# High and low activations in one moving operand, and the MLP's activations moved by 192 bytes

## The chip, the cores and the metric

The kernel runs on one core of one Trainium2 chip. The metric is the device time of one execution in microseconds, the median of several. The profile is that of one execution.

## What is computed

The reference is one layer of a hybrid decoder over 256 tokens of width 2048, in float32:

```python
h = rms_norm(x, pre_mix_norm[l])
gq, gk, gv, gz, ga, gb, mq, mk, mv = jnp.split(h @ w_in[l], split_at, axis=-1)
y_gdn = gdn_branch(gq, gk, gv, gz, ga, gb, conv_w[l], a_log[l], dt_bias[l], gdn_norm_w[l])
y_moba = moba_branch(mq, mk, mv)
mix = jnp.concatenate([y_gdn, y_moba], axis=-1) @ w_out[l]
x = x + rms_norm(mix, post_mix_norm[l])
ca = memory_cross_attention(rms_norm(x, pre_mem_norm[l]), rms_norm(mem, mem_kv_norm[l]),
                            w_mq[l], w_mk[l], w_mv[l], w_mo[l])
x = x + rms_norm(ca, post_mem_norm[l])
f = jnp.square(jax.nn.relu(rms_norm(x, pre_mlp_norm[l]) @ w_up[l])) @ w_down[l]
x = x + rms_norm(f, post_mlp_norm[l])
```

The mixer has 8 heads of a gated delta rule (with a short convolution and silu on q, k and v) and 8 heads of causal softmax attention (one block of 256 tokens). The cross attention has 4 heads over 256 memory tokens, the MLP a hidden width of 8192.

## The kernel before

**Products in parts.** Every matrix product runs in float32r in three parts: each float32 operand is split into a high part, its cast to float32r, and a low part, what is left of it. The product is high x high + high x low + low x high. The weights come from memory in units of 512 KB ([128 partitions, 1024 columns] of float32), in the order of their use (`Stream`, lines 53 to 83): a load on the queue of SP, the cast to the high part `whi` on ScalarE (line 69), the subtraction that gives the low part `wlo` on VectorE (line 71). There are five buffers of raw units and four each of high and low parts, and units are issued three ahead of the one in use.

**Two kinds of product.** In a transposed product the weights are the stationary operand and the activations the moving one, so the result is [128 columns of the product, 256 tokens]. `a_tile` (line 107) makes one such tile of 128 columns in 16 steps, one for each block of 128 rows; `a_group` (line 118) makes four tiles at once, row block by row block, while the activations still arrive. Each step is `three` (line 102): the high weights times the high activations `act[0][k]`, the high weights times the low ones `act[1][k]`, the low weights times the high ones, each with 256 moving columns. In an untransposed product, `b_group` (line 134), the activations are stationary and 512 columns of weights move; it also has three matmuls a step.

Transposed products are: the mixer's k, q, v, z projections and q, k of its block attention (activations x0), the memory's k (activations m0) and q (activations h1) of the cross attention, and all of the MLP's first matrix (activations h2). Untransposed are the attention's v, both output projections, the memory's v and the MLP's second matrix.

**Activations.** `xslot` (line 226) makes two tiles of [128, 16, 256] for high and low parts. `norm_split` (line 222) fills them: the high part on ScalarE, the low part on VectorE. The results of the MLP's first matrix, after relu and square (`up_out`, line 894), are split in the same way into four tiles of eight blocks, one named f and three named fp, which the second matrix reads as stationary operands.

**What takes the tiles out of the banks.** Each tile of a transposed product ends in half a bank, [128, 256]. In the mixer one VectorE instruction multiplies it by the tokens' scales and writes it out: line 341 for k, q and v (`normed`), lines 689 and 690 for the block attention, line 698 for z; line 826 does it for the memory's k, ScalarE's line 863 for the queries of the cross attention. In `up_out` ScalarE's relu reads the bank, VectorE squares, ScalarE casts the high part and VectorE subtracts for the low one.

**Order.** TensorE's order is written by hand: after each unit of weights `tick` lets each generator in the list `bg` do its next step (Gram matrices, the triangular inverse, the delta rule, the softmaxes, transposes of a residual), so its small products stand between the units. On the other engines a scheduler sets the order.

Of the kernel before, what the change touches and what calls it, by code (L numbers as in the profile page):

```python
# [7 lines left out]
F32 = mybir.dt.float32  # L8
F32R = mybir.dt.float32r
I32 = mybir.dt.int32  # L10
AF = mybir.ActivationFunctionType
OP = mybir.AluOpType
# [24 lines left out]
def layer(ctx, tc, xT, xn, memT, cols, rows, wab, win, wout, wmq, wmk, wmv, wmo, wup, wdn, out):  # L37
# [15 lines left out]
    class Stream:  # L53
        """the weights in the order of their use, loaded and split in two float32r parts ahead of it"""
# [47 lines left out]
    def three(o, whi, wlo, act, k, first, last):  # L102
        mm(o, whi, act[0][k], start=first, stop=False)
        mm(o, whi, act[1][k], start=False, stop=False)
        mm(o, wlo, act[0][k], start=False, stop=last)

    def a_tile(act):
        """128 columns, transposed: [column, token]"""
        o = mmps()[:, :T]
        k = 0  # L110
        while k < KT:
            for w in ws.next():
                three(o, *w, act, k, k == 0, k == KT - 1)
                k += 1
            tick()
        return o

    def a_group(act, order, pre=None):
        """512 columns, transposed, over rows as they arrive"""
        o = [mmps()[:, :T] for _ in range(4)]  # L120
# [13 lines left out]
    def b_group(act, kts, last=False, banks=None):  # L134
        """512 columns, as they are: [token, column], the tokens in two blocks"""
# [37 lines left out]
    def newton8(a, name, quarter=None):  # L173
        """-8 / sqrt(a) for columns of sums: each step leaves -2 times its estimate"""
# [50 lines left out]

    def xslot(name):
        hl = [ap_.tile([P, KT, T], F32R, tag="x" + i, name=name + i) for i in "hl"]
        return [[a[:, k] for k in range(KT)] for a in hl]
# [14 lines left out]

    def row_load(pool, tag, i):
        """a norm's weights on every partition, for the scale that newton8 leaves"""
# [17 lines left out]
    def col_sum(sq, name):  # L263
        """1 / root mean square by token, from squares [column, token] summed over the blocks of columns"""
# [6 lines left out]
    hx = xslot("x0")  # L271
    with tc.tile_pool(name="ld", bufs=1) as ld:
# [29 lines left out]
        def ab_tile():  # L302
# [3 lines left out]
            for k in range(KT):  # L306
                three(o, wa[1][:, k], wa[2][:, k], hx, k, k == 0, k == KT - 1)
# [18 lines left out]
    with tc.tile_pool(name="p1", bufs=1) as p1:  # L326
# [11 lines left out]
        def normed(o):  # L338
            c = xcs[count[0] % 4]
            count[0] += 1  # L340
            V.tensor_tensor(c[:, 3:], o, r0b[0], OP.mult)
            return c

        def conv_silu2(c, ch, dst):
            """twice the silu of the convolved channels"""
# [17 lines left out]
        def square_sums(x, dst, h):  # L363
            """the sums over the channels, for each token: columns h and H + h of dst"""
# [81 lines left out]
        def inverse():  # L446
            """the inverses of the 32 x 32 diagonal blocks of I - N, then of the 64s and the 128s"""
# [57 lines left out]
        def level(j0):  # L505
# [3 lines left out]
            for l in range(2):  # L509
                # left: the columns of the first block of each pair, right: those of the second  # L510
# [60 lines left out]
        def gate_rows(q):  # L571
            """the heads' outputs by the inverse root of their mean squares, four heads at a time"""
# [82 lines left out]
        def begin(o_ab):  # L655
            """what follows from the first group once the tokens' scales are there"""
# [18 lines left out]
        for what, h in TURNS:  # L675
# [11 lines left out]
            if what == "m":  # L687
                q, k = t1(), t1()
                V.scalar_tensor_tensor(q, a_tile(hx), QS, r0b[0], OP.mult, OP.mult)
                V.tensor_tensor(k, a_tile(hx), r0b[0], OP.mult)  # L690
# [4 lines left out]
            if what == "z":  # L695
                o = a_tile(hx)
                zs[h] = zt[:, h] if h < 5 else t1()
                V.tensor_tensor(zs[h], o, r0b[0], OP.mult)
# [9 lines left out]
    xp = ctx.enter_context(tc.tile_pool(name="xp", bufs=1))  # L708
    x1 = xp.tile([P, KT, T], F32, tag="x1", name="x1")
    with ExitStack() as es:  # L710
# [6 lines left out]
        def stat_out(o, c, dst, copy):  # L717
            """the squares' sums of 512 columns, and the columns themselves out of the way"""
# [7 lines left out]
        def residual(src, last, wcol, ncol, act, name, lag):  # L726
            """x1 += rms norm of [src, last], transposed; its split for the next product"""
# [299 lines left out]
```

## Time and profile before

| | us |
|---|---|
| median of 3 runs | 1337.73 |
| lowest and highest of them | 1337.37, 1339.63 |
| span of the profiled execution | 1334.2 |
| TensorE matmuls, busy | 1313.6 |
| VectorE, busy | 836.7 |
| ScalarE, busy | 646.8 |

The profiled execution has one span, from its first to its last instruction. It is 3.5 us below the median of the runs, which also holds what lies around it. A matmul's end is modelled, and matmuls overlap, so two rows of matmuls are read by the distance of their starts. The profile names instructions by line, by the tile written and by the tiles read: `mm<-h2h,whi` is a matmul into a bank mm from the high activations h2h and the high weights whi.

### The profile page before, as it was taken

Reading aid. Unit: us, or ns where it says so; the run is one execution under the profiler, and the core shown is the slowest. Engines: PE = TensorE matmul, PEld = TensorE weight load, DVE = VectorE, ACT = ScalarE, POOL = GpSimd, SP = SyncE. Lnnn points to the kernel's source line nnn. Section 1 sums busy time; section 2 is a strip of 40 time slices with the busy share of each in tenths; the row PEclk is TensorE's granted clock in tenths of the full one; section 3 lists DMA queues with packets and bytes.
Section 4 is the critical chain, followed back from the end, with each engine's and each line's share of the span. In section 5 each row is a group of like instructions: output and inputs, shape, how many; then the busy total and the mean of one; then the engine's idle time right before and its main releaser. Section 6 shows DMA issues by size and latency. Waiting matters only on the chain.

```text
span 1334.2 us, 22207 instructions
## 1 busy us (share of the span) xinstructions
PE 1313.6 (98%) x8845; PEld 1211.1 (91%) x8845; DVE 836.7 (63%) x1408; ACT 646.8 (48%) x975; POOL 35.3 (3%) x64
## 2 busy tenths in 40 slices
PE   7999999999999999999999999999999999999996
PEld 7899989999997889889999998888899999888886
DVE  8887769767565769669755554444455555554555
ACT  7544444425445756667544444344444444443442
POOL 1010010100000000000000000000000000000000
PEclk9999999999999999999999999999999999999998
DMA  8465555724347855535555555555555555655552
GB/s 309 159 183 176 187 187 166 206 96 143 129 157 277 283 184 187 207 126 185 188 181 185 180 188 187 191 188 189 188 184 182 186 180 187 217 189 190 189 187 86
DMA packets 72248, 246.49 MB, mean 185 GB/s; under 512 B 10392, under 2 KB 11728, under 8 KB 71760
## 3 DMA queue, kind: packets, MB, share of 16 engines
q1 hardware_dynamic: 69872, 239.27, 54.2%
q0 software_dynamic: 2272, 5.80, 1.7%
q8 instruction: 69, 1.13, 0.3%
q14 instruction: 35, 0.29, 0.1%
HBM read 241.35 MB, written 3.69 MB: 184 GB/s over the span
## 4 chain that ended last, share of the span: by engine, by line
PE 93%; DMA 3%; DVE 2%; ACT 1%; issue 1%; SPq 0%; DVEq 0%; ACTq 0%; POOLq 0%
PE mm L49 86%; PE ax L49 7%; DMA xs<-in_memT_dram 1%; DVE wlo L71 0%; PE ax L750 0%; ACT whi L69 0%; DMA wraw<-in_wout_dram 0%; DMA t<-rd 0%; DVE ca L950 0%; DMA wraw<-in_win_dram 0%; DMA rd<-t 0%; ACT m0h L223 0%; SPq L713 0%; PE ax L620 0%; PE ax L540 0%
## 5 line engine op out<-in xcount | busy, mean ns | idle before, releaser
L71 DVE TENSOR_TENSOR wlo<-wraw,whi 128x1024 fp32r<-128x1024 f32 (+1 forms) x434 | 528.2, 1219 | 372.2 <-ACT whi L69 371.7
L69 ACT ACTIVATE whi<-wraw 128x1024 fp32r<-128x1024 f32 (+1 forms) x434 | 455.3, 1052 | 497.4 <-PE mm L49 282.1
L49 PE MATMUL mm<-h2h,whi 128*128 128x256 f32 x1024 | 290.3, 283 | 0.0
L49 PE MATMUL mm<-h2l,whi 128*128 128x256 f32 x1024 | 289.9, 283 | 0.0
L49 PE MATMUL mm<-h2h,wlo 128*128 128x256 f32 x1024 | 289.9, 283 | 0.0
L49 PE MATMUL mm<-whi,fp 128*128 128x512 f32 (+1 forms) x816 | 244.0, 382 | 0.0
L49 PE MATMUL mm<-x0h,whi 128*128 128x256 f32 x768 | 223.6, 291 | 6.8 <-ACT whi L69 6.8
L49 PE MATMUL mm<-x0h,wlo 128*128 128x256 f32 x768 | 218.3, 284 | 0.0
L49 PE MATMUL mm<-x0l,whi 128*128 128x256 f32 x768 | 218.2, 284 | 0.0
L49 PEld LDWEIGHTS mm<-h2l,whi 128*128 128x128 f32 x1024 | 196.6, 192 | 0.1
L49 PEld LDWEIGHTS mm<-h2h,whi 128*128 128x128 f32 x1024 | 196.6, 192 | 0.0
L49 PEld LDWEIGHTS mm<-h2h,wlo 128*128 128x128 f32 x1024 | 196.6, 192 | 0.0
L49 PEld LDWEIGHTS mm<-whi,fp 128*128 128x128 f32 x816 | 149.9, 188 | 32.6
L49 PE MATMUL mm<-wlo,fp 128*128 128x512 f32 (+1 forms) x408 | 155.7, 382 | 0.0
L49 PEld LDWEIGHTS mm<-x0h,whi 128*128 128x128 f32 x768 | 148.2, 193 | 7.3 <-ACT whi L69 6.8
L49 PEld LDWEIGHTS mm<-x0l,whi 128*128 128x128 f32 x768 | 148.3, 193 | 0.5
L49 PEld LDWEIGHTS mm<-x0h,wlo 128*128 128x128 f32 x768 | 148.1, 193 | 0.2 <-DVE wlo L71 0.2
L49 PEld LDWEIGHTS mm<-wlo,fp 128*128 128x128 f32 x408 | 76.7, 188 | 16.2
L49 PE MATMUL mm<-whi,f 128*128 128x512 f32 (+1 forms) x272 | 81.1, 377 | 0.0
L49 PEld LDWEIGHTS mm<-whi,f 128*128 128x128 f32 x272 | 50.1, 188 | 9.6
L897 ACT ACTIVATE fp<-ft 128x256 fp32r<-128x256 f32 x48 | 20.0, 418 | 65.1 <-DVE ft L896 65.1
L49 PE MATMUL mm<-wlo,f 128*128 128x512 f32 (+1 forms) x136 | 51.3, 378 | 0.0
(368 smaller groups left out, 1445.9 us busy)
## 6 DMA issues: line engine op xcount, KB each, us to landing
wraw<-in_wup_dram SPq DMA_DIRECT2D x128, 512.0 KB, 4.2
wraw<-in_wdn_dram SPq DMA_DIRECT2D x128, 512.0 KB, 3.9
wraw<-in_win_dram SPq DMA_DIRECT2D x110, 512.0 KB, 4.3
wraw<-in_wout_dram SPq DMA_DIRECT2D x32, 512.0 KB, 4.8
wraw<-in_wmk_dram SPq DMA_DIRECT2D x8, 512.0 KB, 4.3
wraw<-in_wmq_dram SPq DMA_DIRECT2D x8, 512.0 KB, 3.8
wraw<-in_wmv_dram SPq DMA_DIRECT2D x8, 512.0 KB, 4.8
wraw<-in_wmo_dram SPq DMA_DIRECT2D x8, 512.0 KB, 4.0
```

Of the source, the lines that this page charges most:

```text
L49: TE.matmul(o, l, r, start=start, stop=stop, skip_group_check=skip)
L69: cast = S.activation(hi, r, AF.Copy)
L71: sub = V.tensor_tensor(lo, r, hi.bitcast(F32), OP.subtract)
L897: S.activation(f[:, 0, j], t, AF.Copy)
```

## The change

A pair of activations now lies side by side: `xslot` makes one tile [128, 16, 2, 256], in which the high and the low 256 columns of a row block follow each other, and `parts` hands out three views of it, high, low, and both as 512 columns. `three` has two matmuls: the high weights times both, 512 columns, into a whole bank, and the low weights times the high activations, 256 columns, onto its left half. The right half then holds high weights x low activations. Whatever takes a tile out of its bank first has ScalarE copy the right half (`right`) and VectorE add the left half to it. In `up_out` the copy stands in the relu's place, and the relu and the square are one VectorE instruction. The small product of the decays, `ab_tile`, keeps its three matmuls. A tile of 48 float32 (192 bytes in each partition) ahead of the MLP's buffers moves them: the three fp tiles' addresses leave 64 bytes over a multiple of 256 where they left 128. The addresses of f, of the inputs' tiles and of the weights' buffers leave 64 before and after.

```diff
     def three(o, whi, wlo, act, k, first, last):
-        mm(o, whi, act[0][k], start=first, stop=False)
-        mm(o, whi, act[1][k], start=False, stop=False)
-        mm(o, wlo, act[0][k], start=False, stop=last)
+        mm(o, whi, act[2][k], start=first, stop=False)
+        mm(o[:, :T], wlo, act[0][k], start=False, stop=last)
+
+    def right(o):
+        t = sm.tile([P, T], F32, tag="right", name="right", bufs=2)
+        S.activation(t, o[:, T:], AF.Copy)
+        return t
...
-        o = mmps()[:, :T]
+        o = mmps()
...
-        o = [mmps()[:, :T] for _ in range(4)]
+        o = [mmps() for _ in range(4)]
...
+    def parts(*tiles):
+        ks = [a[:, k] for a in tiles for k in range(a.shape[1])]
+        return [[k[:, 0] for k in ks], [k[:, 1] for k in ks], [k.rearrange("p i t -> p (i t)") for k in ks]]
+
     def xslot(name):
-        hl = [ap_.tile([P, KT, T], F32R, tag="x" + i, name=name + i) for i in "hl"]
-        return [[a[:, k] for k in range(KT)] for a in hl]
+        return parts(ap_.tile([P, KT, 2, T], F32R, tag="x", name=name))
...
+    def scaled(dst, o, by, const=1.0):
+        t = right(o)
+        V.tensor_tensor(t, o[:, :T], t, OP.add)
+        V.scalar_tensor_tensor(dst, t, const, by, OP.mult, OP.mult)
...
-            V.tensor_tensor(c[:, 3:], o, r0b[0], OP.mult)
+            scaled(c[:, 3:], o, r0b[0])
...
-                V.scalar_tensor_tensor(q, a_tile(hx), QS, r0b[0], OP.mult, OP.mult)
-                V.tensor_tensor(k, a_tile(hx), r0b[0], OP.mult)
+                scaled(q, a_tile(hx), r0b[0], QS)
+                scaled(k, a_tile(hx), r0b[0])
...
-                V.tensor_tensor(zs[h], o, r0b[0], OP.mult)
+                scaled(zs[h], o, r0b[0])
...
-            V.tensor_tensor(km[:, h], a_tile(hm), rmb, OP.mult)
+            scaled(km[:, h], a_tile(hm), rmb)
...
-            S.activation(qm[:, h], om[h], AF.Copy)
+            V.tensor_tensor(qm[:, h], om[h][:, :T], right(om[h]), OP.add)
...
         def up_out(o, t, f, j):
-            S.activation(t, o, AF.Relu)
-            V.tensor_tensor(t, t, t, OP.mult)
+            u = right(o)
+            V.tensor_tensor(t, o[:, :T], u, OP.add)
+            V.scalar_tensor_tensor(t, t, 0.0, t, OP.max, OP.mult)
...
     p3 = ctx.enter_context(tc.tile_pool(name="p3", bufs=1))
+    p3.tile([P, 48], F32, name="pad", tag="pad")
```

On TensorE, where the block attention's first head begins, the last step of a tile, that head's scores and the first step of the next tile stood so (mm_2483 and mm_2572 are the banks of the two tiles, x0h and x0l the high and low activations, t1 the head's q and k):

```order
L49 MATMUL mm_2483<-x0h_84,whi_2410 128x256
L49 MATMUL mm_2483<-x0l_85,whi_2410 128x256
L49 MATMUL mm_2483<-x0h_84,wlo_2412 128x256
L49 MATMUL ax_2556<-t1_2331,t1_2330 128x128
L49 MATMUL ax_2556<-t1_2331,t1_2330 128x256
L49 MATMUL mm_2572<-x0h_84,whi_2446 128x256
L49 MATMUL mm_2572<-x0l_85,whi_2446 128x256
L49 MATMUL mm_2572<-x0h_84,wlo_2448 128x256
```

Now the same place on TensorE reads like this (x0 is the one tile of activations):

```order
L49 MATMUL mm_2183<-x0_84,whi_2123 128x512
L49 MATMUL mm_2183<-x0_84,wlo_2125 128x256
L49 MATMUL ax_2240<-t1_2057,t1_2056 128x128
L49 MATMUL ax_2240<-t1_2057,t1_2056 128x256
L49 MATMUL mm_2259<-x0_84,whi_2151 128x512
L49 MATMUL mm_2259<-x0_84,wlo_2153 128x256
```

Nothing has moved there against the small products; each step has a matmul less. On VectorE, a little ahead of that, the first of the two tiles (the head's q) was taken out of its bank in one instruction, among those of the triangular inverse (ntb) and the subtractions of the weights:

```order
L480 TENSOR_TENSOR t1_2403<-ntb_534 64x112
L689 SCALAR_TENSOR_TENSOR t1_2330<-mm_2332,x0b_564 128x256
L482 TENSOR_TENSOR ntb_534<-ntb_534,t1_2403 64x28x4
L71 TENSOR_TENSOR wlo_2412<-wraw_2408,whi_2410 128x1024
L480 TENSOR_TENSOR t1_2438<-ntb_534 64x135
```

Now VectorE first adds the halves of the bank, and three instructions of the inverse stand between that and the scaling:

```order
L257 TENSOR_TENSOR right_2116<-mm_2058,right_2116 128x256
L498 TENSOR_TENSOR t1_2110<-ntb_469 64x87
L500 TENSOR_TENSOR ntb_469<-ntb_469,t1_2110 64x29x3
L498 TENSOR_TENSOR t1_2113<-ntb_469 64x112
L258 SCALAR_TENSOR_TENSOR t1_2056<-right_2116,x0b_499 128x256
L500 TENSOR_TENSOR ntb_469<-ntb_469,t1_2113 64x28x4
L71 TENSOR_TENSOR wlo_2153<-wraw_2149,whi_2151 128x1024
```

The addition waits for ScalarE's copy of the right half, and the subtraction for the next unit (wlo_2153) stands behind both. On ScalarE the copy stands ahead of the cast of a later unit.

## Rows read from the trace of the kernel before

**Rows 1.** The page: busy us, share of the span and instructions of each engine

```profile
PE 1313.6 (98%) x8845; PEld 1211.1 (91%) x8845; DVE 836.7 (63%) x1408; ACT 646.8 (48%) x975; POOL 35.3 (3%) x64
```

**Rows 2.** Waits of TensorE: who waited for whom, us in total, times, longest

```profile
PE mm L49 <- ACT whi L69: 6.8, 1, 6.8
PE mm L49 <- DVE wlo L71: 1.4, 2, 0.8
```

**Rows 3.** The chain in order of time: start us, us, what, xcount

```profile
46.00 1.36 PE ax L49 x6
...
89.65 17.26 PE mm L49 x144
```

**Rows 4.** Groups by line and form: out<-in, shapes xcount, busy us, mean ns, idle

```profile
L49 PE MATMUL mm<-h2h,whi 128*128 128x256 f32 x1024 | 290.3, 283 | 0.0
...
L49 PE MATMUL mm<-whi,fp 128*128 128x512 f32 x720 | 228.9, 396 | 0.0
L49 PE MATMUL mm<-x0h,whi 128*128 128x256 f32 x768 | 223.6, 291 | 6.8 <-ACT whi L69 6.8
...
L49 PE MATMUL mm<-h1yg,whi 128*128 128x256 f32 x64 | 18.3, 285 | 0.0
...
L49 PE MATMUL mm<-whi,fp 128*128 128x256 f32 x96 | 17.8, 277 | 0.0
```

**Rows 5.** Timeline of TensorE over f: start us, us, what, xcount

```profile
786.00 0.61 PE L49 MATMUL mm<-whi,f 128*128 128x512 f32 x2
...
786.68 0.61 PE L49 MATMUL mm<-whi,f 128*128 128x512 f32 x2
```

**Rows 6.** The same over fp, with 512 columns

```profile
800.45 0.63 PE L49 MATMUL mm<-whi,fp 128*128 128x512 f32 x2
...
801.15 0.63 PE L49 MATMUL mm<-whi,fp 128*128 128x512 f32 x2
```

**Rows 7.** The same over fp, with 256 columns, in the last output group

```profile
1295.35 0.39 PE L49 MATMUL mm<-whi,fp 128*128 128x256 f32 x2
...
1295.69 0.39 PE L49 MATMUL mm<-whi,fp 128*128 128x256 f32 x2
```

**Rows 8.** The same over f, where 512 and 256 columns meet (x2 may hold both)

```profile
1283.32 0.50 PE L49 MATMUL mm<-whi,f 128*128 128x512 f32 x2
1283.66 0.28 PE L49 MATMUL mm<-wlo,f 128*128 128x256 f32 x1
...
1284.86 0.52 PE L49 MATMUL mm<-whi,f 128*128 128x256 f32 x2
1285.21 0.40 PE L49 MATMUL mm<-wlo,f 128*128 128x512 f32 x1
```

**Rows 9.** Groups by line and form, what takes a tile out of its bank

```profile
L895 ACT ACTIVATE ft<-mm 128x256 f32<-128x256 f32 x64 | 23.3, 365 | 0.2 <-PE mm L49 0.2
...
L341 DVE TENSOR_TENSOR xc<-mm,x0b 128x256 f32<-128x256 f32 x24 | 9.9, 423 | 12.2 <-PE mm L49 12.1
```

**Rows 10.** Waits of all engines, the second longest

```profile
ACT whi L69 <- PE mm L49: 282.1, 169, 4.4
```

**Rows 11.** Stretches: busy us (x) of PE, PEld, DVE, ACT, POOL; clock, DMA share, GB/s

```profile
202.00:250.00 48.00, 48.00 (x400) 47.85 (x399) 46.69 (x108) 19.49 (x31) 1.93 (x3) 1.00 0.54 172
491.00:529.00 38.00, 38.00 (x323) 38.00 (x322) 36.82 (x76) 26.79 (x45) 2.15 (x4) 1.00 0.56 182
...
650.00:780.00 130.00, 130.00 (x1086) 130.00 (x1085) 72.38 (x90) 60.61 (x90) 0.00 (x0) 1.00 0.56 183
```

**Rows 12.** Groups of VectorE from 202 to 250 us, the tiles of k

```profile
L690 DVE TENSOR_TENSOR t<-mm,x0b 128x256 f32<-128x256 f32 x4 | 1.6, 409 | 0.0
```

**Rows 13.** Groups of VectorE from 491 to 529 us, the tiles of the memory's k

```profile
L826 DVE TENSOR_TENSOR km<-mm,mmb 128x256 f32<-128x256 f32 x4 | 1.7, 421 | 0.0
```

**Rows 14.** The stretch of the first output projection, columns as in rows 11

```profile
404.00:455.00 51.00, 49.51 (x216) 39.95 (x215) 36.49 (x53) 35.59 (x55) 1.64 (x3) 1.00 0.77 282
```

**Rows 15.** The chain in the same stretch: start us, us, what

```profile
414.81 11.44 DMA xs<-in_memT_dram
```

More of the change, by code (lines that the diff above doesn't have):

```diff
@@ L306, in ab_tile @@
             for k in range(KT):
-                three(o, wa[1][:, k], wa[2][:, k], hx, k, k == 0, k == KT - 1)
+                mm(o, wa[1][:, k], hx[0][k], start=k == 0, stop=False)
+                mm(o, wa[1][:, k], hx[1][k], start=False, stop=False)
+                mm(o, wa[2][:, k], hx[0][k], start=False, stop=k == KT - 1)
             return o
@@ L818, in layer @@
         km = p2c.tile([P, HM, T], F32, name="km")
-        yb = [ap_.tile([P, 2, H, T], F32R, tag=t, name="h1" + t) for t in ("yg", "ym")]
-        h1 = [[a[:, i, k] for i in range(2) for k in range(H)] for a in yb]
+        h1 = parts(*[ap_.tile([P, H, 2, T], F32R, tag=t, name="h1" + t) for t in ("yg", "ym")])
         bg.append(residual(mix, om, n_sc[:, 0], n_pmem, h1, "x1", 1))
@@ L921, in layer @@
         else:
-            wrow = row_load(ap_, "xl", 2)
+            wrow = row_load(ap_, "x", 2)
             fw = {}
```

## The prediction

> **What bounds the kernel now.** I read the busy times first, then the waits of TensorE, then the spacing of its matmuls. TensorE is busy for 98% of the span, VectorE for 63%, ScalarE for 48% [rows 1]; a busy share of pipelined matmuls alone says little, so the waits come next. TensorE waits for weights 6.8 us at the start, before anything can run, and 1.4 us later [rows 2]. That is nearly all: from the first weights to the last product the kernel is as long as the sum of the distances between its matmuls. So the price of a matmul is its distance to the next one, not the duration printed for it (283 ns for one that the next follows after 120 ns [rows 3, 4]).
>
> Two rows of the chain give these distances in undisturbed stretches: 144 matmuls of 256 columns in 17.26 us, 119.9 ns each, and six of 512 columns (in the attention's v) in 1.36 us, 226.7 ns each [rows 3]. Twice the columns cost 1.89 times as much: from the two, a matmul costs 106.8 ns for 256 columns and 13.1 ns that do not depend on the columns. The second part is what a change that merges two matmuls can win.
>
> The products over the MLP's activations show a second thing. Where the stationary operand is in f, three matmuls of 512 columns take 0.68 us [rows 5]; where it is in fp, 0.70 us [rows 6], 233.3 ns each. With 256 columns it is the other way round: three in fp take 0.34 us, 113.3 ns each [rows 7], not 119.9. In the built program the addresses of the weights' buffers, of the inputs' tiles and of f all leave 64 bytes over a multiple of 256, those of fp leave 128. That is the only difference that I see between the two.
>
> **The change, part by part.** *One wide matmul for two.* A step of a transposed product (one block of 128 rows) had three matmuls of 256 columns, 359.6 ns. Now it has one of 512 and one of 256: 226.7 + 119.9 = 346.6 ns, 13.0 ns less. The steps are counted by their first matmul: 1024 over h2, 768 over the first input, 64 over the memory and 64 over h1 (the row of h1yg; memory has as many) [rows 4]: 1920 steps, **25.0 us**. No stretch before has the two sizes in turn all along, so the pair is bounded from both sides by rows: 226.7 + 113.3 = 340 ns with the cheap kind of each, 233.3 + 119.9 = 353 ns with the dear kind. At the changes of size in the last output group, over f, a wide matmul and the narrow one behind it take 0.34 us, a narrow one and the wide one behind it 0.35 us [rows 8]. These lie on both sides of 346.6, and the stream's addresses there are those that the new steps have; I take 346.6. The bounds give 12.7 us to 37.6 us.
>
> The Trainium skill's page "TensorE: Matmul & The Clock Gate", section "Back-to-back issue gap", gives a matmul at the full clock N/2.4 + 2.5 ns. By it one matmul fewer per step is worth an estimated 4.8 us in all. The trace does not agree: its distances are some 11 ns above that rule for both sizes.
>
> *The 192 bytes.* They bring fp to the remainder of f. 1080 matmuls of 512 columns over fp (720 with the high weights [rows 4], half as many with the low) go from 233.3 to 226.7 ns, which gains 7.1 us; 144 of 256 columns (96 and half as many) go from 113.3 to 119.9 ns, which loses 1.0 us. Together **6.1 us**. If the remainder is not the cause, 0.
>
> *What it adds.* The result now lies in two halves of a bank that must be added. For 48 tiles of the mixer (4 first, 12 k and q, 8 v, 8 z, 16 of the block attention) and 4 of the memory, one VectorE instruction becomes two and ScalarE gets a copy out of the bank; in the MLP's 64 tiles ScalarE's relu becomes that copy, and VectorE gets one instruction more; for the 4 queries of the cross attention ScalarE's copy stays and VectorE gets one more. By rows that is 0.42 us of VectorE for each of 120 tiles, 50 us, and 0.365 us of ScalarE for 52, 19 us [rows 9]. They cost the time only where TensorE comes to wait for them. The work that hides them is TensorE's own. The casts of the weights on ScalarE stood idle for 282.1 us until a matmul gave a buffer back [rows 10], so the weights' parts lie ready in front of TensorE. In the MLP, VectorE has 72.38 us of work in 130 [rows 11]; its 22 or so tiles there (130 / 5.75) add 9 us.
>
> Two stretches have no such cover: 202 to 250 us (VectorE busy 46.69 of 48, under the triangular inverse) and 491 to 529 us (36.82 of 38, under the first residual) [rows 11]. The tiles evicted there, 8 (four k, and four q beside them) and 4 [rows 12, 13], add 3.4 and 1.7 us to a full engine, while TensorE gets faster by 0.2 us a tile. At most these 5 us come through, at least nothing, as the engine was full before without a wait of TensorE's.
>
> *The new wait.* ScalarE's copy waits for the end of a tile, VectorE's add for the copy. Behind the copy stands the cast of a later unit of weights, behind the add its subtraction, as the order shows, and TensorE waits for both in the end. In the MLP the relu waited in the same place, so nothing is new there; in the mixer it was VectorE alone that waited. I take **3 us** for all of it (0 to 8): half of the full stretches, and a little at the inverse and the delta rule, where each tile's VectorE chain is now 0.8 us longer.
>
> *What is not touched.* From 404 to 455 us the weights arrive at the pace of the transfers (282 GB/s) [rows 14], behind a load of the residual that waits until the mixer's buffers are free, and a transfer of 11.44 us ends a wait in the chain [rows 15]. A faster TensorE reaches this place earlier, and the place moves with it; it is made of untransposed products, which the change leaves as they are. The end, from the last products to the stores, stays too.
>
> *Sum.* 1334.2 - 25.0 - 6.1 + 3 = 1306.1 us of span. The median of the runs lies 3.5 us above the profiled span (1337.73 against 1334.2), and I keep that: **1309.6 us**, 2.1% less.
>
> **The rivals.** *The dear pair.* The wide matmul keeps the 233.3 ns that it has after a change of size and the narrow one its 119.9: 6.6 ns a step, 12.7 us, and 1309.6 + 12.3 = 1321.9. For it: 0.35 us for one order of the two. Against it: 0.34 us for the other, and a wide one has to stand in both orders.
>
> *The cheap pair.* 340 ns, 37.6 us: 1297.0. It has the same rows for and against it, with the sides changed.
>
> *It does not do what it says.* If the time of a matmul goes by its columns, nothing is gained by merging: the columns of a step are 768 before and after. At 119.9 ns for 256 the step stays at 359.6 ns. Then 1309.6 + 25.0 = 1334.6 us with the addresses' share. Against it stands that 512 columns do not take 239.8 ns in the trace, but 226.7.
>
> *Slower: VectorE sets the pace.* The added instruction of each tile stands in VectorE's queue ahead of a subtraction of weights. If the subtractions come late by that much at every tile, TensorE waits 0.42 us 120 times, 50 us: 1306.6 + 50 = 1357 us. It decides from 31.1/120 = 0.26 us a tile on, where all gains are eaten. For it speaks that VectorE is full in two stretches; against it, that these hold 12 of the 120 tiles, and that TensorE waited 1.4 us for the low parts in the whole run [rows 2].
>
> **How the numbers follow.** A difference of 0.2%, 2.7 us, is about what a measurement of this kernel can tell from no change, so faster means below 1335.1 us and slower above 1340.4. I give the forecast 0.74, the dear pair 0.09, the cheap pair 0.06, no gain by merging 0.05 and VectorE's pace 0.06. The first three are faster, and so would no gain by merging be, but by 0.5 us only, so I count it as 0.01 faster and 0.04 same. VectorE's pace would be same in part of its course: 0.01 same, 0.05 slower. Faster 0.90, same 0.05, slower 0.05. The range: a pair of 343 ns and no stall give 1337.7 - 31.9 - 6.1 = 1299.7; a pair of 351 ns and stalls of 8 us give 1337.7 - 16.5 - 6.1 + 8 = 1323.1. I take 1299 to 1323, which reaches over the dear pair too.
>
> **What would show it right or wrong.** In the MLP's first half a tile of 16 steps should take 5.55 us where it took 5.75, the pair of matmuls 0.347 us; the products over fp 0.68 us for three. The waits of TensorE for the low parts should stay below some 5 us in all, and those that are new should lie around 200 to 300 and 490 to 530 us. Pairs near 0.34 or 0.353 us mean one of the first two rivals. A subtraction of weights that TensorE waits for tile after tile, and VectorE in the chain with several per cent, mean the last. Three matmuls over fp that still take 0.70 us mean that the remainder of the address is not the cause. The prediction is wrong if a stretch that had no wait gets one that comes back at every tile.

## The result and the profile after

| | before | after |
|---|---|---|
| median of 4 runs each, us | 1337.55 | 1323.62 |
| lowest to highest, us | 1337.00 to 1339.63 | 1321.07 to 1325.81 |
| profiled execution, us | not known | 1325.32 |
| its span, us | 1334.2 | 1323.6 |

The ratio is 0.9891, with a 95% interval from 0.9877 to 0.9905. The kernel became 13.9 us faster. The direction is the predicted one. The time lies at the upper end of the range (1299 to 1323) and 0.6 us past it, and the gain is half of the 28.1 us that were forecast. The two profiled spans differ by less, 10.6 us: the changed kernel's four runs lie in two pairs, 1321.1 and 1321.9 us at a mean granted clock of 0.997 and 0.996 and 1325.3 and 1325.8 us at 0.994, and the profile is that of the run of 1325.3 us (0.0025 of the clock are an estimated 3.3 us in 1323). Wherever both are known, the time of a run is 1.7 to 1.9 us above its span. So the span of 1334.2 us belongs to an execution of about 1336 us, and the 3.5 us that the prediction adds to a span compare two different executions; the forecast gain does not depend on them.

The first line of the page of the changed kernel answers to [rows 1]:

```profile
PE 1298.4 (98%) x6925; PEld 1111.2 (84%) x6925; DVE 875.9 (66%) x1528; ACT 663.0 (50%) x1027; POOL 35.4 (3%) x64
```

There are 1920 matmuls fewer, one for each step that was counted. VectorE has 39 us more to do and ScalarE 16 us.

TensorE's waits in the changed kernel (who waited for whom, us in total, times, longest) answer to [rows 2]:

```profile
PE mm L49 <- ACT whi L69: 9.5, 2, 6.5
PE ax L49 <- ACT t L560: 1.6, 1, 1.6
PE ax L49 <- DVE t L258: 1.1, 2, 0.8
...
PE ax L49 <- DVE ym L648: 0.7, 1, 0.7
PE mm L49 <- DVE wlo L71: 0.5, 1, 0.5
```

The 6.5 us are the start, as before. New are a wait of 3.0 us for high weights in the output projection (9.5 less 6.5), and two kinds of waits of the small products (ax), for ScalarE's line 560 and VectorE's line 258; a third kind (ym) grew from 0.4 to 0.7 us. All three lie between 220 and 315 us. The low weights, which the slower rival named, account for 0.5 us.

The new pair of matmuls in the timeline of TensorE, in the middle of the MLP's first half (start us, us, what):

```profile
639.63 0.40 PE L49 MATMUL mm<-h,whi 128*128 128x512 f32 x1
639.87 0.28 PE L49 MATMUL mm<-h,wlo 128*128 128x256 f32 x1
...
642.81 0.40 PE L49 MATMUL mm<-h,whi 128*128 128x512 f32 x1
```

From 639.63 to 642.81 there are nine pairs: 3.18 us, **353.3 ns a pair**. The forecast took 346.6; this is the price of the dear rival. But the kernel has both prices. By the starts in its trace, 1656 of the 1920 pairs lie 353.3 ns apart, among them all of the MLP's, and 192 lie 346.7 ns apart, all of them between the small products from 222 to 397 us (the other 72 lie in two stretches that begin at the lower clock, at 6 and at 294 us). Here are twelve of the 192, 4.16 us from the first row to the last:

```profile
388.30 0.39 PE L49 MATMUL mm<-x,whi 128*128 128x512 f32 x1
...
392.46 0.39 PE L49 MATMUL mm<-x,whi 128*128 128x512 f32 x1
```

Behind the first pair or two, the price of the changed kernel stays the same within a stretch that no small product breaks. Over fp the distances are those that the prediction gave. With 512 columns:

```profile
797.16 0.62 PE L49 MATMUL mm<-whi,fp 128*128 128x512 f32 x2
...
797.84 0.62 PE L49 MATMUL mm<-whi,fp 128*128 128x512 f32 x2
```

Three matmuls take 0.68 us, where [rows 6] show 0.70. With 256 columns, in the last output group:

```profile
1292.86 0.40 PE L49 MATMUL mm<-whi,fp 128*128 128x256 f32 x2
...
1293.21 0.40 PE L49 MATMUL mm<-whi,fp 128*128 128x256 f32 x2
```

Three take 0.35 us, where [rows 7] show 0.34. Both forms went to the distances over f.

Where the time went is seen from the distances between the first matmuls of the stages. The table also has three of the kernels that are told of below: the old evictions under the new matmuls (e6), and two with another order of the matmuls (e5, e12).

| us from the first matmul of a stage to that of the next | before | after | e6 | e5 | e12 |
|---|---|---|---|---|---|
| from the first m tile to the delta rule's first product (10 m and 1.5 v tiles, under the triangular inverse) | 73.4 | 73.7 | 72.5 | 72.3 | 71.7 |
| from there to the output projection (delta rule; 6.5 v, the last 6 m and 3 z tiles) | 129.9 | 131.2 | 126.9 | 128.5 | 130.7 |
| output projection | 91.3 | 95.5 | 91.9 | 96.6 | 90.0 |
| MLP, first half, up | 186.2 | 182.7 | 182.8 | 180.1 | 180.1 |
| MLP, first half, down | 178.0 | 174.1 | 174.1 | 174.1 | 174.1 |
| MLP, second half, up | 184.3 | 180.9 | 180.9 | 178.1 | 178.1 |
| MLP, second half, down | 177.8 | 175.5 | 175.5 | 175.5 | 175.5 |

After the change the MLP is 13.1 us faster; the output projection, which the change leaves as it is, takes 4.2 us more, and the two stages ahead of it lose 1.6 us although their products got cheaper.

### The profile page after: what moved, and what is told of

Read it like the earlier page. It is cut to its first block, busy times and chain, and to the rows that moved or that the text cites. A ratio compares the mean times of both kernels' runs of the same rounds, so it can differ in the third digit from the quotient of the medians.

```text
span 1323.6 us, 18597 instructions
## 1 busy us (share of the span) xinstructions
PE 1298.4 (98%) x6925; PEld 1111.2 (84%) x6925; DVE 875.9 (66%) x1528; ACT 663.0 (50%) x1027; POOL 35.4 (3%) x64
## 4 chain that ended last, share of the span: by engine, by line
PE 91%; DVE 4%; DMA 3%; ACT 1%; issue 1%; SPq 0%; DVEq 0%; POOL 0%; ACTq 0%; POOLq 0%
PE mm L49 84%; PE ax L49 7%; DMA wraw<-in_wout_dram 1%; DVE wlo L71 1%; ACT whi L69 1%; PE ax L768 0%; DMA t<-rd 0%; DVE ca L969 0%; DVE t L498 0%; DVE ntb L500 0%; DMA wraw<-in_win_dram 0%; DMA cbk<-ccd 0%; DMA ccd<-t 0%; DMA rd<-t 0%; PE ax L874 0%
## 5 line engine op out<-in xcount | busy, mean ns | idle before, releaser
L49 PE MATMUL mm<-h,whi 128*128 128x512 f32 x1024 | 362.5, 399 | 0.0
L49 PE MATMUL mm<-h,wlo 128*128 128x256 f32 x1024 | 287.6, 281 | 0.0
L49 PE MATMUL mm<-x,whi 128*128 128x512 f32 x768 | 280.2, 407 | 6.5 <-ACT whi L69 6.5
L49 PEld LDWEIGHTS mm<-h,whi 128*128 128x128 f32 x1024 | 192.4, 188 | 48.1 <-DVE h L230 0.2
L49 PE MATMUL mm<-x,wlo 128*128 128x256 f32 x768 | 216.8, 282 | 0.0
L49 PEld LDWEIGHTS mm<-h,wlo 128*128 128x128 f32 x1024 | 193.5, 189 | 0.0
L49 PEld LDWEIGHTS mm<-x,whi 128*128 128x128 f32 x768 | 146.0, 190 | 39.9 <-ACT whi L69 6.5
L49 PEld LDWEIGHTS mm<-x,wlo 128*128 128x128 f32 x768 | 146.6, 191 | 1.3 <-DVE wlo L71 0.8
L49 PEld LDWEIGHTS mm<-wlo,fp 128*128 128x128 f32 x408 | 76.8, 188 | 13.9
L49 PE MATMUL mm<-whi,ym 128*128 128x512 f32 x128 | 43.4, 400 | 3.0 <-ACT whi L69 3.0
L110 ACT ACTIVATE right<-mm 128x256 f32<-128x256 f32 x120 | 43.7, 368 | 4.2 <-PE mm L49 2.9
```

The lines of the kernel that those rows point to most:

```text
L49: TE.matmul(o, l, r, start=start, stop=stop, skip_group_check=skip)
L110: S.activation(t, o[:, T:], AF.Copy)
```

## Experiments

Two questions were open: why a pair costs 353.3 ns, and what the added evictions cost. In each experiment the ratio is to the runs of the kernel before that were made beside it (medians 1337.1 to 1337.5 us).

**e1: the 192 bytes alone.** The kernel before, with one line added:

```
     p3 = ctx.enter_context(tc.tile_pool(name="p3", bufs=1))
+    p3.tile([P, 48], F32, name="pad", tag="pad")
```

> The kernel before with the 192 bytes alone; the transposed products keep three matmuls of 256 columns. If the address remainder of fp is the cause of its 233.3 ns, the products over fp go to 227 ns (512 columns) and 120 ns (256 columns), as over f, and the time falls by 6.1 us to 1331.5 us (ratio 0.9955). If it is not the cause, both spacings stay at 233 and 113 ns and the time stays within 1 us of the kernel before. The changed kernel has the 227 ns, so that the first is likely; open is whether the 6 us come through without the other part of the change.

Measured: 1330.47 us (1330.06 to 1332.33), ratio 0.9950 (0.9935 to 0.9965), against 1337.09 for the kernel before: **6.6 us** less. The timeline over fp in this kernel:

```profile
799.78 0.61 PE L49 MATMUL mm<-whi,fp 128*128 128x512 f32 x2
...
800.46 0.61 PE L49 MATMUL mm<-whi,fp 128*128 128x512 f32 x2
```

Three matmuls take 0.68 us. With 256 columns three take 0.36 us, where [rows 7] show 0.34. Moving the buffer by 192 bytes is enough for that; nothing else is different from the kernel before.

**e2: eight wide matmuls, then eight narrow ones.** The changed kernel with another order inside a unit of weights:

```
-            for w in ws.next():
-                three(o, *w, act, k, k == 0, k == KT - 1)
-                k += 1
+            u = ws.next()
+            wides([o], u, [slice(0, P)], act, list(range(KT)), k)
+            k += len(u)
...
+    def wides(o, u, cs, act, order, n):
+        for i, w in enumerate(u):
+            for b, c in zip(o, cs):
+                mm(b, w[0][:, c], act[2][order[n + i]], start=n + i == 0, stop=False)
+        for i, w in enumerate(u):
+            for b, c in zip(o, cs):
+                mm(b[:, :T], w[1][:, c], act[0][order[n + i]], start=False, stop=n + i == KT - 1)
```

> The changed kernel, but of each unit of weights the eight wide matmuls first, then the eight narrow ones, instead of wide and narrow in turn. Theory A (each change of size costs, and in turn the two never settle): eight wide at some 230 ns and eight narrow at some 119 ns, 349 ns a pair instead of 353.3, 1920 steps by 4.3 ns = 8 us less than the changed kernel, 1315.5 us; at most 346.6 ns a pair, 12.9 us less, 1310.7 us. Theory B (the dear pair is due to the addresses of the activations and the weights, in whatever order): a pair stays at 353 ns and the time within 1.5 us of the changed kernel's 1323.6.

Measured: 1316.58 us (1316.13 to 1317.09), ratio 0.9844 (0.9828 to 0.9861), 7.0 us less than the changed kernel. Its timeline, eight matmuls to a row:

```profile
642.15 2.00 PE L49 MATMUL mm<-h,whi 128*128 128x512 f32 x8
643.99 1.12 PE L49 MATMUL mm<-h,wlo 128*128 128x256 f32 x8
...
653.32 2.00 PE L49 MATMUL mm<-h,whi 128*128 128x512 f32 x8
```

From 642.15 to 653.32 there are 32 pairs in 11.17 us, 349.1 ns each. Theory A gave 349, theory B 353. So the order of the sizes changes the price of the same matmuls at the same addresses, here in the MLP. The added evictions are all still there, and yet TensorE waits only 0.6 us for high weights in the output projection, which takes 91.2 us: what the evictions cost depends on the order too.

**e3 and e4: the activations at other addresses.** Two small tiles in the pool move the tile of the activations, and put everything behind it back (e4 has 16 and 48 in place of 48 and 16):

```
+    ap_.tile([P, 48], F32, name="pa", tag="pa")
     hx = xslot("x0")
+    ap_.tile([P, 16], F32, name="pb", tag="pb")
```

> The changed kernel with the tile of the activations, high and low parts, moved by 192 bytes to remainder 0 of 256 (it leaves 64 in the changed kernel); nothing else is moved. Theory A (order of sizes): the pair stays at 353 ns, within 1 ns, and the time at 1323 us, within 2. Theory B (addresses): the pair changes by 3 ns or more to either side, up to the 340 or 360 ns of the bounds, and the time by 5 us or more (1792 of the 1920 steps read this tile).

> The changed kernel with the tile of the activations moved by 64 bytes to remainder 128 of 256, the one that fp had before the change. Theory A: 353 ns a pair, within 1, and 1323 us, within 2. Theory B: by the spacings over fp before the change, 233 ns for the wide and 113 for the narrow, 346 ns a pair, 1792 steps by 7 ns = 12.5 us less, 1311 us; or another change of 3 ns or more.

Measured: 1327.52 us in e3 (1327.13 and 1327.90) and 1322.51 in e4 (1320.38 and 1324.63), two runs each. The rows of both, e3 first:

```profile
639.68 0.40 PE L49 MATMUL mm<-h,whi 128*128 128x512 f32 x1
...
642.86 0.40 PE L49 MATMUL mm<-h,whi 128*128 128x512 f32 x1
```

```profile
639.76 0.39 PE L49 MATMUL mm<-h,whi 128*128 128x512 f32 x1
...
642.94 0.39 PE L49 MATMUL mm<-h,whi 128*128 128x512 f32 x1
```

Nine pairs take 3.18 us in both, 353.3 ns as in the changed kernel: in the MLP's first half a pair in turn costs the same at all three remainders. In e4's second half it does not, although the tile and its address are the same as in the first:

```profile
1040.30 0.40 PE L49 MATMUL mm<-h,whi 128*128 128x512 f32 x1
...
1046.93 0.39 PE L49 MATMUL mm<-h,whi 128*128 128x512 f32 x1
```

From 1040.30 to 1046.93 there are 19 pairs in 6.63 us, 348.9 ns each, and the whole up stage of this half is 2.3 us shorter than in the changed kernel. So neither theory is enough: the sizes in turn stand at 346.7, 348.9 or 353.3 ns a pair, more than one of them at one address, and what decides which a stretch takes is open. e3's time misses "1323, within 2" by 2.5 us. Its MLP takes as long as that of the changed kernel, so this is not the pair's. Its trace has the 3.0 us wait of the changed kernel's trace and the lower clock at the same two places (0.79 from 292 to 300 us; 0.69 from 430 to 441 us), and the two spans, 1325.4 and 1323.6 us, differ by 1.8 us only.

e4 tells something of the 192 bytes too. In the attention's v the tile of the activations is the stationary operand; at remainder 128, the one that fp had before the change, three of its matmuls take 0.70 us, as those over fp did:

```profile
181.24 0.63 PE L49 MATMUL mm<-whi,x 128*128 128x512 f32 x2
...
181.94 0.63 PE L49 MATMUL mm<-whi,x 128*128 128x512 f32 x2
```

In the changed kernel, at 64, they take 0.68 us.

**e5: half as many changes of size.** In every second unit of a tile the narrow ones come first:

```
+        turned = n // len(u) % 2 == 1
+        for wide in ((0, 1) if turned else (1, 0)):
```

> The kernel with eight wide matmuls, then eight narrow ones per unit of weights, but in every second unit of a tile the narrow ones first: 8 wide, 16 narrow, 8 wide, so that the size changes half as often. Theory A (what a pair costs above 346.6 ns is paid at the changes of size): the 2.7 ns a pair that were left at eight are halved, 348.0 ns a pair, 1920 by 1.3 ns = 2.6 us less than with eight in one order (1316.6), 1314 us. Rival: it is paid once per unit of weights, whatever the order; then it stays at 1316.6, within 1.

Measured: 1315.96 us (1315.43 to 1318.96), ratio 0.9848 (0.9834 to 0.9863). The timeline:

```profile
645.30 2.08 PE L49 MATMUL mm<-h,wlo 128*128 128x256 f32 x16
647.21 3.82 PE L49 MATMUL mm<-h,whi 128*128 128x512 f32 x16
650.86 2.08 PE L49 MATMUL mm<-h,wlo 128*128 128x256 f32 x16
...
656.43 0.76 PE L49 MATMUL mm<-h,wlo 128*128 128x256 f32 x5
```

32 pairs in 11.13 us, 347.8 ns: the pair is what theory A gave (348.0), and both up stages are 0.5 or 0.6 us shorter than with eight in one order. The time fell by 0.6 us only, not by 2.6, so that by the time alone the rival (1316.6, within 1) would hold: TensorE leaves the delta rule sooner (128.5 us where eight in one order had 131.9), and loses more in the output projection (96.6 where that kernel had 91.2).

**e6: the new matmuls with the old evictions.**

```
-            u = right(o)
-            V.tensor_tensor(t, o[:, :T], u, OP.add)
-            V.scalar_tensor_tensor(t, t, 0.0, t, OP.max, OP.mult)
+            S.activation(t, o[:, :T], AF.Relu)
+            V.tensor_tensor(t, t, t, OP.mult)
```

(and so in `scaled` and for the four queries).

> The changed kernel with its wide and narrow matmuls as they are, but with the evictions of the kernel before: the right half of the banks (high weights by low activations) is computed and left out of the result, ScalarE's copy and VectorE's add are gone. Theory A (the added evictions cost only in the stretches without cover, and the pair is dear by itself): pairs stay at 353.3 ns, the MLP's up stretches at 182.7 and 180.9 us, and only the stalls between 195 and 400 us go, 2 to 4 us, with up to 4 us more in the output projection if its late weights are a consequence of the added copies: 1316 to 1321 us. Rival (the evictions disturb the matmuls all along, and so make the pair dear): pairs of 347 ns, up stretches of 178 us, 1311 us or less.

Measured: 1315.45 us (1314.36 to 1317.24), ratio 0.9841 (0.9825 to 0.9857): **8.2 us** less than the changed kernel. By the two ratios it is 6.7 us, and each of them is known to about 2 us. TensorE's waits between 192 and 480 us in this kernel:

```profile
PE mm L49 <- DVE wlo L71: 1.4, 2, 0.8
PE mm L49 <- ACT whi L69: 0.4, 1, 0.4
PE ax L556 <- DVE t L567: 0.3, 1, 0.3
```

The three kinds of waits of the small products and the 3.0 us for high weights are gone. In the MLP nothing is gained (up stages 182.8 and 180.9, as with the evictions), so the evictions neither stall TensorE there nor make the pair dear. By the table, 1.2 us of the gain lie under the inverse, 4.3 at the delta rule, 3.6 in the output projection (the two profiled spans differ by 9.7 us).

The output projection shows how an eviction in one stage is paid in the next. Its loads of weights wait for buffers that VectorE's subtractions give back; among the waits of the DMA queue from 385 to 440 us of the changed kernel this is by far the longest:

```profile
SPq L67 <- DVE wlo L71: 30.7, 8, 8.3
```

These subtractions stand in one queue with VectorE's last work on the mixer. The first row of each pair is the first matmul of the output projection, the second the last gate of the mixer on VectorE; first the kernel before, then the changed one, then e6:

```profile
398.18 0.47 PE L49 MATMUL mm<-whi,ym 128*128 128x512 f32 x1
...
410.36 1.09 DVE L651 TENSOR_TENSOR yg<-t,yg 128x256 fp32r<-128x256 f32 x3
```

```profile
396.64 0.48 PE L49 MATMUL mm<-whi,ym 128*128 128x512 f32 x1
...
411.69 0.42 DVE L669 TENSOR_TENSOR yg<-t,yg 128x256 fp32r<-128x256 f32 x1
```

```profile
391.57 0.48 PE L49 MATMUL mm<-whi,ym 128*128 128x512 f32 x1
...
403.64 1.10 DVE L667 TENSOR_TENSOR yg<-t,yg 128x256 fp32r<-128x256 f32 x3
```

The gate ends 13.3 us after the projection's begin before the change, 15.5 after it and 13.2 with the old evictions. TensorE reached the projection 1.5 us earlier, VectorE's last step came 0.7 us later. The other runs fit this: over all fourteen traces the gate ends 12.4 (e12) to 17.2 us (e5) after the projection's begin and the projection takes 90.0 to 96.6 us, but from the gate's end to the projection's end it is always 76.2 to 80.1 us. So the projection's end goes with the gate's end more closely than with TensorE's begin; e2, with 15.0 and 91.2 us, fits least. Around the gate's end the transfers stand still. That was so before (first row, in the columns of [rows 11]), but TensorE had more weights in hand:

```profile
406.00:409.00 3.00, 3.00 (x15) 2.46 (x14) 3.00 (x8) 0.89 (x2) 0.00 (x0) 1.00 0.00 0
```

In the changed kernel loads of weights, of the residual's input and of the memory are all due together after the pause, and TensorE has used up its lead at 427.5 us. Its windows:

```profile
405.00:409.00 4.00, 4.00 (x19) 3.31 (x18) 4.00 (x10) 2.18 (x5) 0.00 (x0) 1.00 0.13 13
...
426.00:430.00 4.00, 1.53 (x7) 0.94 (x5) 0.48 (x1) 2.01 (x5) 0.00 (x0) 1.00 1.03 413
430.00:437.00 7.00, 5.98 (x13) 4.41 (x14) 5.79 (x9) 7.00 (x13) 0.00 (x0) 0.51 0.59 174
437.00:441.00 4.00, 4.00 (x19) 3.27 (x19) 3.97 (x5) 2.45 (x5) 0.00 (x0) 1.00 0.94 349
```

Behind the wait of 3.0 us the granted clock is 0.51, the lower level (1.2 GHz), for the next 7 us. TensorE is busy for 5.98 of them, at half speed, so that some 3 us more are lost: the wait costs as much again after its end. That the added evictions cost these 8.2 us in this order of the matmuls is shown by e6; the way over VectorE's queue is read from the traces and was not tried by itself. A smaller loss of the same kind stands in e1, which has no added evictions: a wait of 1.2 us for high weights, a granted clock of 0.66 from 432 to 437 us behind it, and 92.9 us for the projection.

**e7: the residual's input later.** The changed kernel; the four loads go from ahead of the projection's weights to between them:

```
-        for q in range(4):
-            nc.sync.dma_start(x1[:, 4 * q:4 * q + 4], xT[q])
...
                 stat_out(om, c, mix, lambda d, s: S.activation(d, s, AF.Copy))
+                for q in {1: (3, 0), 2: (1, 2)}.get(c, ()):
+                    nc.sync.dma_start(x1[:, 4 * q:4 * q + 4], xT[q])
```

> The changed kernel, but the four loads of the residual's input are issued later: two after the second column group of the output projection and two after the third, instead of all four ahead of the projection's weights. Theory A (the 3 us wait of TensorE for weights at 428 us, and the half clock after it, come from these 2 MB ahead of the weights): the wait and the 6.8 us of half clock are gone, the output projection takes 89 to 91 us instead of 95.5, the runs no longer fall in two groups (1321 and 1325.5), 1317 to 1319 us. Rival (the transfers are at their pace anyway, or the weights wait for ScalarE's casts): the stage stays above 94 us and the time at 1322 to 1325 us.

Measured: 1325.09 us (1324.52 to 1326.67), ratio 0.9914 (0.9899 to 0.9929), no gain. The waits from 400 to 492 us in this kernel, and the window behind the former wait:

```profile
PE mm L49 <- DVE wlo L71: 3.5, 5, 0.8
PE mm L49 <- ACT whi L69: 0.9, 1, 0.9
```

```profile
430.00:437.00 7.00, 6.24 (x27) 4.75 (x26) 4.38 (x5) 4.53 (x8) 0.00 (x0) 1.00 0.94 310
```

The long wait and the half clock are gone, but waits for the low weights of one unit after another take their place, and the stage stays at 95.3 us. So moving these 2 MB behind the first weights does not save the loss, as theory A had it; the waits read as if the pause of the transfers cost the same in one piece or in several.

**e8: e5 and e7 together.**

> The order of eight wide, sixteen narrow, eight wide, and the later loads of the residual's input, together. If both gains are real and independent: 1316.6 - 2.6 for the order, and 0 to 4 us for the loads (with eight in one order the output projection took 91.2 us already): 1310 to 1314 us. If the loads merely move the rush to another place, 1314 us or more.

Measured: 1316.04 us (1315.42 to 1318.64), ratio 0.9848 (0.9833 to 0.9863), as e5 alone. The output projection takes 96.4 us. The later loads give nothing in this order either.

**e9, e11, e12: which tiles the added evictions hurt.** e5, but some tiles of the mixer go back to three matmuls of 256 columns and the old eviction:

```
+                for n, (whi, wlo) in enumerate(u, k):
+                    mm(o[:, :T], whi, act[0][n], start=n == 0, stop=False)
+                    mm(o[:, :T], whi, act[1][n], start=False, stop=False)
+                    mm(o[:, :T], wlo, act[0][n], start=False, stop=n == KT - 1)
...
+        if not side:
+            return V.scalar_tensor_tensor(dst, o[:, :T], const, by, OP.mult, OP.mult)
```

> The kernel with 8 wide, 16 narrow, 8 wide, but the 27 tiles of the mixer after the second mv group (16 of the block attention, 8 v, the last 3 z) go back to three matmuls of 256 columns and to one VectorE instruction as eviction, as before the change. Theory A (the 8 us that the added evictions cost arise at these tiles, under the inverse and the delta rule): 27 x 16 steps x 11.6 ns = 5.0 us are given up and some 7 to 8 us won back: 1312 to 1314 us, against 1316.0 with all tiles wide; TensorE's waits at 220 and 290 to 372 us and the half clock behind them are gone, and the output projection takes 91 to 93 us. Rival (the loss comes from the evictions of the tiles before, or from the output projection's loads alone): 1319 to 1321 us.

> As the kernel with 27 tiles back at three matmuls, but only the 16 tiles of the block attention (m) go back; the 8 v and the last 3 z are wide, with their added evictions. If the cost of the added evictions arises at the m tiles, under the inverse at 200 to 250 us: the 11 tiles gain 11 x 16 x 11.6 = 2.0 us, 1311 us. If it arises at v and z, under the delta rule: the waits at 290 to 372 us, the late weights of the output projection and the half clock come back, 1315 to 1318 us.

> The other half: the 8 v and the last 3 z tiles go back to three matmuls of 256 columns and their old evictions, the 16 m tiles are wide. If the loss arises at v and z alone: all waits stay away and the 16 m tiles gain 16 x 16 x 11.6 = 3.0 us over the kernel with 27 tiles back (1312.9), 1310 us. If m and v and z only fill the engines together (either half is enough to make the output projection's weights late): a wait of 2 to 3 us near 428 us with half clock behind it, 1314 to 1317 us.

| tiles that go back | us, median of 4 | ratio (95%) | output projection, us | pair gain given up, us |
|---|---|---|---|---|
| none (e5) | 1315.96 | 0.9848 (0.9834 to 0.9863) | 96.6 | 0 |
| 16 m, 8 v, 3 z (e9) | 1312.89 | 0.9824 (0.9807 to 0.9840) | 91.7 | 5.0 |
| 16 m (e11) | 1316.12 | 0.9846 (0.9830 to 0.9863) | 94.9 | 3.0 |
| 8 v, 3 z (e12) | **1312.04** | 0.9812 (0.9796 to 0.9829) | 90.0 | 2.0 |

The waits between 192 and 480 us, first e11, then e12:

```profile
PE mm L49 <- ACT whi L69: 2.6, 1, 2.6
PE mm L49 <- DVE wlo L71: 1.1, 2, 0.8
```

```profile
PE ax L49 <- DVE t L580: 0.9, 1, 0.9
PE mm L49 <- DVE wlo L71: 0.6, 1, 0.6
```

What the old evictions win back is the fall in time plus the pair gain given up: 3.1 + 5.0 = 8.1 us for all 27 tiles, 2.8 for the m tiles (-0.2 + 3.0), 5.9 for v and z (3.9 + 2.0). The two parts add up to about the whole, and the whole is near the 8.2 us of e6, but each of these figures is known to some 2 us only. A tile that goes back also takes TensorE 0.2 us more, which gives VectorE time; these runs don't separate that from the eviction. With v and z alone the wait for high weights is gone; with m alone it stays. e12 is the fastest kernel of the study, 11.6 us below the changed one and 25.4 below the kernel before beside it.

**e10: one VectorE instruction for copy and add.** e5, with the halves of the bank added by a sum over both:

```
-        t = right(o)
-        V.tensor_tensor(t, o[:, :T], t, OP.add)
+        t = sm.tile([P, T], F32, tag="right", name="right", bufs=2)
+        V.tensor_reduce(t, o.rearrange("p (i t) -> p t i", i=2), AX.X, OP.add)
```

> The kernel with 8 wide, 16 narrow, 8 wide, but in the mixer's and the memory's 52 tiles the two halves of the bank are added by one VectorE instruction that reads both (a sum over two columns), without ScalarE's copy. Theory A (the cost in the mixer is the wait of VectorE for ScalarE's copy, behind the casts in its queue): VectorE's work per tile grows by a few tenths of a us, the stalls between 200 and 400 us shrink, 1310 to 1314 us. Theory B (the cost is VectorE's own added time): the stalls stay or grow by the longer instruction, 1316 to 1320 us.

Measured: 1316.39 us (1314.71 to 1316.91), ratio 0.9844 (0.9829 to 0.9858), as e5. Its row by form, and below it that of the add in the changed kernel:

```profile
L260 DVE TENSOR_REDUCE right<-mm 128x256 f32<-128x512 f32 x52 | 35.6, 687 | 24.1 <-PE mm L49 24.0
```

```profile
L257 DVE TENSOR_TENSOR right<-mm,right 128x256 f32<-128x256 f32 x52 | 21.6, 416 | 0.3 <-ACT right L110 0.2
```

Without the wait for ScalarE, but with 0.27 us more of VectorE's own time a tile, the time stays. TensorE's wait for the scaled tile under the inverse grows from 0.3 us (e5) to 2.1:

```profile
PE ax L49 <- DVE t L261: 2.1, 2, 1.2
```

That agrees with theory B; but two things change at once, and the run doesn't separate them.

## Why the prediction was right and wrong

*The bound: right.* The time still follows the distances between matmuls, and the stages whose matmuls became cheaper became shorter, except where a wait took its place.

*The pair: merging does save time, but its size was wrong.* The step that failed reads "These lie on both sides of 346.6 [...]; I take 346.6". It took the price of two sizes in long runs of their own for the one price in turn. Measured in turn, 1656 of 1920 pairs stand at 353.3 ns and only 192 at the forecast price: 6.3 instead of 13.0 ns for most steps, and 12.1 us if all 1920 are counted so, instead of 25.0. Merging by itself brought 21.8 - 6.6 = 15.2 us (e6 against e1), some 3 us more. Of these, e6's 160 pairs at 346.7 ns make 1.1 us, and an estimated 0.8 us comes from the steps before the change, which take 360.0 ns in the MLP (184.3 us for the 512 of its second half) and not 359.6; the rest is within what these medians can tell. Why most stretches stand at 353.3 ns is open. [rows 8] could not decide the price: they have a hundredth of a us for differences of 7 ns, and hold only the first rows after a change of size. The dear pair was a rival with nearly the right price for most pairs, at a chance of 0.09. Its reason stands in no row, since the 233.3 ns are those of the wide matmuls over fp and not those behind a change of size; that its 1321.9 us lies near to what was measured is partly luck, as it had 5 us too little for the evictions and some 2.5 us too little for the merging.

The rule that the Trainium skill's page "TensorE: Matmul & The Clock Gate", section "Back-to-back issue gap", gives for a matmul by itself (N/2.4 + 2.5 ns at the full clock) makes an estimated 325 ns of a pair. The trace does not agree: no stretch of pairs here stands below 346.7 ns. These are streams with a load of weights for each matmul (6925 of both in the changed kernel), for which the section says that the rule gives too little at few columns and too much at many; the prediction left that out. Here it gives too little at both sizes, 216 and 109 ns where 226.7 and 119.9 were measured.

*The 192 bytes: right.* 6.1 us forecast, 6.6 measured (e1), with both spacings as given.

*The added evictions: too small, and at the wrong place.* Forecast 3 us (0 to 8), measured 8.2 (e6). The added work was 39 us on VectorE and 16 on ScalarE, where 50 and 19 were forecast; that was not the fault. Of the two full stretches that the prediction named, the second (491 to 529 us) cost nothing: TensorE has no wait there. The first, with its surroundings, cost 1.2 us. The rest lies where the prediction had "a little", at the delta rule, and where it had nothing. The failed step is "What is not touched. From 404 to 455 us [...] A faster TensorE reaches this place earlier, and the place moves with it". By the traces the place does not move with TensorE but with VectorE's last step of the mixer, which came 0.7 us later while TensorE came 1.5 us earlier. In the MLP "nothing is new there" holds: 83.96 us of VectorE in 130 instead of 72.38 [rows 11], with no wait:

```profile
650.00:780.00 130.00, 130.00 (x738) 112.70 (x737) 83.96 (x136) 62.63 (x94) 0.00 (x0) 1.00 0.59 187
```

*The rivals.* The cheap pair (340 ns) and no gain by merging (359.6 ns) are refuted, as no stretch stands below 346.7 ns or above 353.3 at the full clock. VectorE setting the pace is refuted too: TensorE waited 0.5 us for low weights in all.

*The balance.* Forecast 28.1 us; 9.8 less from the pair (25.0 to 15.2), 5.2 less from the evictions (3 to 8.2), 0.5 more from the address: 13.6, and 13.9 were measured. Each item is a difference of medians that is known to some 2 us, so the agreement to 0.3 is luck.

## What to carry to other kernels

Take the price of a mixed stream from a long stretch of a mixed stream, and look at more than one stretch: here two sizes in turn took 346.7, 348.9 or 353.3 ns, while runs of eight or sixteen of a size took 349.1 and 347.8 ns in the MLP, where the changed kernel had the 353.3. When a faster engine runs ahead of a slower chain, ask at the next stage whether the loads are paced by the fast engine or by the last step of the slow one. An edit that pays everywhere but in one stretch can be left out of that stretch alone: 11 tiles taken back here, in the kernel with eight wide, sixteen narrow, eight wide, were worth 3.9 us.

## What the hardware showed that was not expected

- A wide and a narrow matmul in turn have no single price. In one stretch it is 353.3, 348.9 or 346.7 ns, for up to 512 pairs without a change: 353.3 in the whole second up stage of the changed kernel (180.9 us for 512 pairs), 348.9 in that of e4 (178.6 us). In e4 both halves of the MLP read the same tile at the same address, and the first stands at 353.3.
- The matmuls over fp changed by 6 to 7 ns either way, 512 columns down and 256 up, when only their stationary operand's remainder changed from 128 to 64 (e1). With the attention's v it is the same the other way round: 0.68 us for three at 64 in the changed kernel, 0.69 at 0 in e3, 0.70 at 128 in e4.
- After TensorE had idled for 3.0 us with all work before it at the full clock, the granted clock was at the lower level for about 7 us (0.51 in the window), so that the wait cost about twice its length. In the changed kernel a wait of 0.7 us among small products stands before another such stretch (the window from 292 to 300 us has 0.79); in e4 the same wait at the same place is followed by the full clock (1.00 in the same window). In e9 and e12, which have no wait above 1 us between 192 and 480 us, the windows from 430 to 437 us have the full clock.
- One VectorE sum over two halves of a bank (512 columns in, 256 out) takes 687 ns, more than half again as long as an add of 256 columns that takes one operand from the bank (416 ns).
